# A decoder layer's down projection: Strassen's block products in place of plain ones

## The chip, the cores and the metric

The kernel runs on one core of a Trainium2 chip. Its metric is the device time of one execution in microseconds. Three executions of the kernel before took 1628.73, 1629.14 and 1631.95 us, median 1629.14 us.

## The reference, cut to what matters

One layer of a decoder over 1024 tokens of 1024 channels, all in float32. After an input projection, two head groups (retention and RWKV-7) and an output projection comes the part that changes, and behind it a gated embedding and a last norm:

```python
x = x + mixed @ w_o
hf = rms_norm(x, norm_ffn_w)
x = x + (silu(hf @ w_gate) * (hf @ w_up)) @ w_down      # hidden width 2816
hp = rms_norm(x, norm_ple_w)
x = x + (p @ w_ple_up) * sigmoid(hp @ w_ple_gate)
return rms_norm(x, final_norm_w)
```

## The kernel before

Channels lie on the 128 partitions and tokens along the free axis, in two halves of 512. Every float32 matrix is split into two float32r parts, hi and lo, that add up to it (`split`, L246: ScalarE copies hi, VectorE or GpSimd subtracts it for lo). A product of two such matrices takes three matmuls: hi by hi, hi by lo, lo by hi. All these matmuls are issued at L189, in `mm`. An accumulation (eviction from PSUM into SBUF) is a VectorE addition with one operand in SBUF and one in PSUM.

`dense` (L255) runs over a list of weight tiles of 128 output channels by 1024: it loads each in two pieces of 512 columns by DMA (`st`), splits them into `hi` and `lo` (three buffers each), makes 24 matmuls, and hands the PSUM tile `d` to a `use` function. It yields after every third matmul. The last argument of `dense` (L1124) says which engine makes `lo` of a weight tile: VectorE for all tiles of the tail.

The tail begins when both head groups are done for the second token half. `out1` adds the output projection of the second half to `x1`, the residual, which stays in SBUF from there; `norm1` makes the operand `hT`. In the list of `dense` the last two tiles of the first half (`ffn0`) stand between `out1` and what follows, and `norm1` is called within the first of them. Then `ffn1` runs over the 22 hidden tiles of the second token half, gate and up in turn: 48 matmuls of `d` for each hidden tile. The first half of the hidden layer was made earlier and lies in DRAM (`hd`).

The hidden tiles go in pairs (FC = 2: eleven parts, counted from 0). `chunk` takes a buffer for the part, `fetch` loads and splits both hidden tiles of the first token half and both row tiles of `w_down`, and `up` splits the second half's hidden tiles as they are made. After a part's second `up` comes `down(c, 0)` and `down(c, 1)`: for each of 8 output tiles and each token half 6 matmuls into one PSUM bank `pd`, and one VectorE addition into `x1` at L1116. That is 96 matmuls and 16 additions a part. The last part's first token half is brought forward to the end of the tenth part, so that its norm has time; its second half stands between the products `pg` of the embedding's gate, whose weights `wg` are loaded by `gate_weights` during parts 6 to 9.

What runs when is set by the order in which the program emits instructions; a scheduler then orders each engine's stream by priority and by its own cost model. Each engine works its stream in order, and SyncE (SP) issues all DMAs, in order too.

Of the kernel before, what the change touches and what calls it, by code (L numbers as in the profile page):

```python
# [8 lines left out]
F32 = mybir.dt.float32  # L9
# [7 lines left out]
P = 128  # L17
# [12 lines left out]
# columns of the packed constants  # L30
# [7 lines left out]
# columns of the packed parameter vectors  # L38
# [43 lines left out]
# a group may enter a stage once the group before it has reached another  # L82
# [95 lines left out]
def tile_hybrid_layer(ctx: ExitStack, tc: tile.TileContext, I, out):  # L178
# [7 lines left out]
    def mm(ps, lhsT, rhs, start, stop):  # L186
        n = math.prod(rhs.shape[1:])
        pe[0] += n / 2.4 if rhs.dtype == F32R else 2 * max(107.0, n / 1.2)
        return nc.tensor.matmul(ps, lhsT, rhs, start=start, stop=stop)  # L189
# [55 lines left out]
    # a float32 value as two float32r parts that add up to it exactly  # L245
# [53 lines left out]
    def rsqrt(y, x, tmp):  # L299
        """y = x ** -0.5 in place of x for positive x: a guess from the exponent, then Newton's steps"""  # L300
# [8 lines left out]
    # RMS norm over the channels, which lie on the partitions  # L309
# [39 lines left out]
    # =================== input norm, input projection, RWKV and retention ===================  # L349
    with ExitStack() as s1:  # L350
# [22 lines left out]
        # x times the norm's weights; 1 / rms comes in when the projections leave PSUM  # L373
# [57 lines left out]
        def lerp(h, ps, i, t):  # L431
            """token shift with mu of tile i, token half h"""
# [35 lines left out]
        def low(h):  # L468
            """decay, in-context rate and gate of all heads from their low-rank parts"""
# [14 lines left out]
            # the high part beside the low one: one pass over 128 rows for both  # L484
# [34 lines left out]
        # block-diagonal holders; the zero blocks are written once  # L519
# [33 lines left out]
        def rwkv_group(p, hf):  # L553
            """a pair of heads over 8 chunks of 64 tokens; yields (stage, ns until the next matmuls can start)"""
# [11 lines left out]
            def headsum(ps, t):  # L566
                """sum of t over the channels of a head"""
# [11 lines left out]
            # decay and normaliser  # L579
# [35 lines left out]
            # products inside the chunks  # L615
# [25 lines left out]
            # inverse of the unit triangular blocks of 32 rows  # L641
# [32 lines left out]
            # two chunks at a time, then each head's rows to their place  # L674
# [20 lines left out]
            # merge to 64 rows  # L695
# [16 lines left out]
            # the chunk as an affine map: S' = P_C (M S + Kf V), y = Q S + Hy V  # L712
# [9 lines left out]
            for g in range(2):  # L722
# [8 lines left out]
                # M and Q take the room of their factor  # L731
# [6 lines left out]
            # the state (before P_C, transposed) and the output: [(h, v), (k | t)] of each chunk  # L738
# [18 lines left out]
            # head norm in token-major form, bonus, gate  # L757
# [34 lines left out]
        def retention(h, a):  # L792
            """a head over four chunks of 128 tokens; yields ns until the next matmuls can start"""
# [26 lines left out]
            # the scores take the room of v, the states that of k, the output that of the token-major k  # L820
# [13 lines left out]
            # the state before each chunk  # L834
# [25 lines left out]
            # (qs y - mean) / sqrt(var + eps) with the moments of y  # L860
# [16 lines left out]
        # =================== the dense products in an order that feeds the groups ===================  # L877
# [3 lines left out]
        # the embedding's operands, in the room of the retention  # L881
# [57 lines left out]
        # the last heads' first token half before their second one: the operands of the output projection take its room  # L939
# [13 lines left out]
        def mix_load(h, k):  # L953
            """operands of the output projection, token half h"""
# [38 lines left out]
        def ffn0(f, then=None):  # L993
            """the first token half of the hidden layer, kept in DRAM"""
# [53 lines left out]

        FC = 2
        NC = NF // FC  # L1050

        def ffn1(f):
            c, i = f // FC, f % FC

            def gate(ps):
                if i == 0 and c < NC - 1:
                    chunk()
                if f in tail["gates"]:
                    tail["gates"][f]()
# [3 lines left out]
                if c < NC - 1:  # L1063
                    fetch(c, 2 * i)

            def up(ps):
                h = tail["s"][i]
                t = hold.pop(f)
                V.tensor_tensor(out=t, in0=t, in1=ps, op=ALU.mult)
# [120 lines left out]
    for _ in dg:  # L1190
        pass
# [132 lines left out]
```

## Time and profile before

The page of the profile is that of one execution whose span was 1630.8 us from first to last instruction; the page gives no other time for that execution, and its span lies among the three times above.

| engine | busy us | share of the span |
| --- | --- | --- |
| TensorE (PE) | 1519.8 | 93% |
| its weight loads (PEld, beside PE) | 1237.5 | 76% |
| VectorE (DVE) | 1118.9 | 69% |
| ScalarE (ACT) | 689.5 | 42% |
| GpSimd (POOL) | 286.4 | 18% |

The mean granted clock of TensorE was 0.983 of full speed. The share of busy time is an average over stages with different limits, so each stage has to be read for itself. The tail lies from about 1033 us on.

### The profile page before, as it was taken

What the parts mean: (1) busy time and instruction counts of PE and PEld (TensorE: products, weight loads), DVE (VectorE), ACT (ScalarE), POOL (GpSimd) and SP (SyncE); (2) the same over time, 40 slices, a digit from 0 to 9 for tenths busy, and PEclk for the clock granted to TensorE, in tenths of its full rate; (3) what the DMA queues carried; (4) which work ended last, traced back from release to release, by engine and by line L of the source; (5) the groups of instructions that cost most, each with busy time, mean ns of one, the idle gap of its engine ahead of it and who ended that gap; (6) DMA issues with size and microseconds to landing.
All of it is one profiled execution on the core that took longest, in us unless ns stands there. A gap on an engine that the chain in (4) does not pass through costs nothing.

```text
span 1630.8 us, 21374 instructions
## 1 busy us (share of the span) xinstructions
PE 1519.8 (93%) x7406; PEld 1237.5 (76%) x7406; DVE 1118.9 (69%) x2364; ACT 689.5 (42%) x1383; POOL 286.4 (18%) x232
## 2 busy tenths in 40 slices
PE   7999999998888889889899999999999999999994
PEld 5777778786766668767677778788888888788894
DVE  7669796959798697894955545855555554556776
ACT  6655444443635547354253234522222222224554
POOL 7410111021222123323233320000000000000012
PEclk9999999999999999999999999999999999999997
DMA  6544242333534655243333545422222223321222
GB/s 204 168 160 154 91 130 82 111 119 101 194 118 130 211 162 176 69 150 101 117 124 111 167 144 171 155 93 85 84 85 82 73 79 97 104 78 46 72 84 78
DMA packets 108763, 194.06 MB, mean 119 GB/s; under 512 B 12272, under 2 KB 16496, under 8 KB 108656
## 3 DMA queue, kind: packets, MB, share of 16 engines
q1 hardware_dynamic: 108656, 192.71, 37.1%
q8 instruction: 58, 0.95, 0.2%
q14 instruction: 49, 0.40, 0.1%
HBM read 151.24 MB, written 41.42 MB: 118 GB/s over the span
## 4 chain that ended last, share of the span: by engine, by line
PE 54%; DVE 25%; DMA 8%; ACT 7%; issue 4%; POOL 2%; SPq 1%; DVEq 0%; ACTq 0%; POOLq 0%
PE d L189 30%; PE pd L189 14%; DVE tmp L643 4%; PE pg L189 3%; DVE R L645 3%; POOL lo L248 2%; DMA st<-in_w_in_dram 1%; DMA st<-in_w_up_dram 1%; ACT hi L247 1%; DVE lo L248 1%; DMA st<-mixd 1%; DVE Dm L637 1%; DMA st<-in_w_gate_dram 1%; PE pb L189 1%; PE pkh L189 1%
## 5 line engine op out<-in xcount | busy, mean ns | idle before, releaser
L189 PE MATMUL d<-hT,hi 128*128 128x512 f32 x1408 | 449.7, 399 | 6.5 <-ACT hi L247 4.0
L189 PE MATMUL d<-x,hi 128*128 128x512 f32 x960 | 322.7, 411 | 9.0 <-ACT x L336 6.7
L247 ACT ACTIVATE hi<-st 128x512 fp32r<-128x512 f32 x298 | 187.6, 629 | 314.0 <-PE d L189 142.7
L189 PEld LDWEIGHTS d<-hT,hi 128*128 128x128 f32 x1408 | 261.5, 190 | 57.8 <-ACT hi L247 6.6
L248 POOL TENSOR_TENSOR lo<-st,hi 128x512 fp32r<-128x512 f32 x139 | 194.1, 1397 | 597.6 <-ACT hi L247 529.6
L189 PE MATMUL d<-hT,lo 128*128 128x512 f32 x704 | 278.7, 396 | 2.8 <-POOL lo L248 2.2
L189 PE MATMUL pd<-h 128*128 128x512 f32 x1056 | 241.8, 389 | 0.0
L189 PEld LDWEIGHTS pd<-h 128*128 128x128 f32 x1056 | 198.2, 188 | 41.1
L189 PEld LDWEIGHTS d<-x,hi 128*128 128x128 f32 x960 | 179.1, 194 | 43.6 <-ACT x L336 6.7
L189 PE MATMUL d<-x,lo 128*128 128x512 f32 x480 | 194.0, 404 | 2.3 <-POOL lo L248 2.3
L248 DVE TENSOR_TENSOR lo<-st,hi 128x512 fp32r<-128x512 f32 x159 | 110.7, 697 | 109.4 <-ACT hi L247 108.9
L1116 DVE TENSOR_TENSOR x<-x,pd 128x512 f32<-128x512 f32 x176 | 120.5, 687 | 92.7 <-PE pd L189 91.8
L189 PEld LDWEIGHTS d<-hT,lo 128*128 128x128 f32 x704 | 133.6, 190 | 35.6 <-POOL lo L248 5.0
L247 ACT ACTIVATE h<-xr 128x512 fp32r<-128x512 f32 x66 | 38.4, 624 | 194.6 <-PE pd L189 176.7
L1198 POOL TENSOR_TENSOR x<-x,xr 128x256 f32<-128x256 f32 (+1 forms) x18 | 19.8, 1130 | 561.6 <-DVE xr L328 561.6
L189 PEld LDWEIGHTS d<-x,lo 128*128 128x128 f32 x480 | 93.1, 194 | 22.1 <-POOL lo L248 4.2
L643 DVE TENSOR_TENSOR tmp<-Dt,R 128x248 f32<-128x248 f32 (+30 forms) x248 | 89.8, 362 | 3.2
L645 DVE TENSOR_TENSOR R<-R,tmp 128x248 f32<-128x248 f32 (+30 forms) x248 | 82.7, 334 | 3.3
L189 PE MATMUL d<-mix,hi 128*128 128x512 f32 x256 | 82.1, 400 | 1.6 <-ACT hi L247 1.5
L189 PEld LDWEIGHTS d<-mix,hi 128*128 128x128 f32 x256 | 48.1, 192 | 11.7 <-ACT hi L247 1.9
L248 DVE TENSOR_TENSOR h<-xr,h 128x512 fp32r<-128x512 f32 x66 | 42.8, 689 | 14.0 <-ACT h L247 13.9
L1004 POOL TENSOR_TENSOR g<-g,R 128x512 f32<-128x512 f32 x22 | 29.2, 1325 | 125.6 <-DVE g L1003 122.8
(284 smaller groups left out, 2159.8 us busy)
## 6 DMA issues: line engine op xcount, KB each, us to landing
st<-in_w_gate_dram SPq DMA_DIRECT2D x88, 256.0 KB, 2.9
st<-in_w_up_dram SPq DMA_DIRECT2D x88, 256.0 KB, 2.8
st<-in_w_in_dram SPq DMA_DIRECT2D x86, 256.0 KB, 2.9
xr<-in_w_down_dram SPq DMA_DIRECT2D x44, 256.0 KB, 3.4
retd<-rt SPq DMA_DIRECT2D x32, 256.0 KB, 2.6
rr<-retd SPq DMA_DIRECT2D x32, 256.0 KB, 3.4
st<-in_w_o_dram SPq DMA_DIRECT2D x32, 256.0 KB, 3.0
rkvd<-rkvt SPq DMA_DIRECT2D x24, 256.0 KB, 2.2
```

Source lines behind the costliest of these rows:

```text
L189: return nc.tensor.matmul(ps, lhsT, rhs, start=start, stop=stop)
L247: act(hi, src, AF.Copy)
L248: (eng or V).tensor_tensor(out=lo, in0=src, in1=hi.bitcast(F32), op=ALU.subtract)
L637: V.tensor_tensor(out=Dm, in0=d0v[:, 0].rearrange("p u t -> p t u").unsqueeze(2).broadcast_to([P, 32, 4, NU]), in1=d0v[:, 1].rearrange("p ...
L643: V.tensor_tensor(out=tmp[:, :, 0:i], in0=Dt[:, i:i + 1, 0:i].broadcast_to([P, 8, i]), in1=R[:, :, i:i + 1].broadcast_to([P, 8, i]), op=AL ...
L645: V.tensor_tensor(out=R[:, :, 0:i], in0=R[:, :, 0:i], in1=tmp[:, :, 0:i], op=ALU.subtract)
L1004: G.tensor_tensor(out=g, in0=g, in1=R0[0], op=ALU.mult)
L1116: V.tensor_tensor(out=x1, in0=x1, in1=ps, op=ALU.add)
L1198: (V if b == S and d % 3 < 2 else G).tensor_tensor(out=x1[d][:, a:b], in0=x1[d][:, a:b], in1=R, op=ALU.mult)
```

## The change

Ten of the eleven parts are no longer multiplied plainly but by Strassen's product in Winograd's form. A part's product is taken as 2 by 2 blocks: the two weight rows by two halves of 512 output channels (A0, A1 for the first half, A2, A3 for the second), the two hidden tiles by two token halves (B0, B1 the first half, from DRAM; B2, B3 the second, just made). Seven block products P1 to P7 of sums of these replace eight. A block product is 4 output tiles (`j`) of one 128-row product: 4 units of 3 matmuls. So a part has 28 units, 84 matmuls, each with its own addition into `x1` or into one of eight new accumulators `E` (E0 to E3 for P1, E4 to E7 for P7), which are added into `x1` once, at the end (`shared`). P2, P7 and P3 go on in the PSUM bank of the product before them, after that has been read.

The units no longer stand in a block behind a part's dense products. `period(c)` makes a table of 32 ticks: one for each yield of `dense` within a part. In period c the units of part c - 1 are emitted, one a tick, while the operands of part c are loaded, summed and split: the weights' sums and the lo parts of their seven operands on GpSimd, those of the first token half on VectorE. At the end of the period `hidden(c)` makes the second half's sums and splits on VectorE. Operands live in a ring of eight slots (tiles ring_9689 and ring_9690); rm_9691 and rm_9692 are E, rm_9693 holds B0, B1 and the weight sums A4, A5, rm_9694 holds B2 to B5, and xr0 to xr3 are A0 to A3. The lo parts of every other dense weight tile of the tail are also made on GpSimd.

The last part stays plain. Its first half, the split of the embedding's operand (`hp_split`) and the last units of part 9 are laid out by `last_period`. The embedding's first four gate weights now go into slots of the ring as these come free, the third and fourth after the dense products.

```diff
+        def weights(c):
...
+            return {-24: lambda: dma(out=A[0], in_=I["w_down"][row(0), half(0)]),
+                    -16: lambda: dma(out=A[2], in_=I["w_down"][row(0), half(1)]),
+                    -9: lambda: dma(out=A[1], in_=I["w_down"][row(1), half(0)]),
+                    -5: lambda: dma(out=A[3], in_=I["w_down"][row(1), half(1)]),
+                    0: lambda: (dma(out=B[0], in_=hd[f]), dma(out=B[1], in_=hd[f + 1])),
+                    1: lambda: (part(c, "P1", 0, A[0], G), sums()),
+                    3: lambda: sub(G, A[2], A[0], A[2]),
...
+                    26: lambda: part(c, names(c)[6], 0, A[3] if names(c)[6] == "P4" else A[1], G)}
+        def hidden(c):
+            B = tail["B"]
+            sub(V, B[4], B[2], B[0])
+            sub(V, B[5], B[3], B[4])
+            part(c, "P6", 1, B[5])
+            sub(V, B[2], B[3], B[2])
+            part(c, "P7", 1, B[2])
+            sub(V, B[1], B[5], B[1])
+            for n in names(c)[4:]:
+                part(c, n, 1, {"P5": B[4], "P3": B[3], "P4": B[1]}[n])
+        def unit(c, name, j):
...
+            for n, (w, x) in enumerate(((0, 0), (0, 1), (1, 0))):
+                mm(ps, t[:, 0, w, cd], t[:, 1, x], start=(first and n == 0), stop=(n == 2), more=not first)
...
+            if c == 0 and name in ("P1", "P7"):
+                act(dst, ps, AF.Copy)
+            else:
+                V.tensor_tensor(out=dst, in0=dst, in1=ps, op=ALU.subtract if name == "P4" else ALU.add)
+        def shared(j):
+            V.tensor_tensor(out=E[4 + j], in0=E[4 + j], in1=E[j], op=ALU.add)
+            V.tensor_tensor(out=x1[j + 4][:, half(0)], in0=x1[j + 4][:, half(0)], in1=E[4 + j], op=ALU.add)
+            G.tensor_tensor(out=x1[j][:, half(1)], in0=x1[j][:, half(1)], in1=E[j], op=ALU.add)
+            G.tensor_tensor(out=x1[j + 4][:, half(1)], in0=x1[j + 4][:, half(1)], in1=E[4 + j], op=ALU.add)
+        def period(c):
+            ticks = [[] for _ in range(32)]
+            if c:
+                for u in range(28):
+                    ticks[u].append(lambda u=u: unit(c - 1, names(c - 1)[u // 4], u % 4))
...
-                    for w, x in ((wh, hh), (wh, hl), (wl, hh)):
-                        mm(ps, w, x, start=(n == 0), stop=(n == 3 * FC - 1))
-                        n += 1
-                x1 = tail["x1"][d][:, half(h)]
-                V.tensor_tensor(out=x1, in0=x1, in1=ps, op=ALU.add)
...
-        dg = dense(items, count, done, lambda i: G if 0 < i < ntail and (i < EV0 or i % EVM) else V)
+        dg = dense(items, count, done, lambda i: G if 0 < i < ntail and (i < EV0 or i % EVM) or i > ntail + KT and i % 2 else V)
...
     for _ in dg:
-        pass
+        tick()
```

TensorE before, in the tail, where a part's dense products (`d`) end and its down products (`pd`) begin:

```order
L189 MATMUL d<-hT_9498,lo 128x512
L189 MATMUL d<-hT_9498,hi 128x512 x2
L189 MATMUL d<-hT_9498,lo 128x512
L189 MATMUL pd<-h 128x512 x96
L189 MATMUL d<-hT_9498,hi 128x512 x2
L189 MATMUL d<-hT_9498,lo 128x512
L189 MATMUL d<-hT_9498,hi 128x512 x2
```

TensorE now, at the end of a middle part; a number behind `pd` is the PSUM tile of one output tile. The first row is the last of P1's four units, and the units that follow are P2's, in the same banks:

```order
L189 MATMUL pd_11833<-ring_9690 128x512 x3
L189 MATMUL d_11809<-hT1_9498,hi_11719 128x512 x2
L189 MATMUL d_11809<-hT1_9498,lo_11720 128x512
L189 MATMUL d_11809<-hT1_9498,hi_11763 128x512 x2
L189 MATMUL d_11809<-hT1_9498,lo_11764 128x512
L189 MATMUL d_11809<-hT1_9498,hi_11763 128x512
L189 MATMUL pd_11802<-ring_9689 128x512 x3
L189 MATMUL d_11809<-hT1_9498,hi_11763 128x512
L189 MATMUL d_11809<-hT1_9498,lo_11764 128x512
L189 MATMUL d_11809<-hT1_9498,hi_11763 128x512
L189 MATMUL pd_11813<-ring_9689 128x512 x3
L189 MATMUL pd_11825<-ring_9689 128x512 x3
```

The down products stand in threes between dense ones, and four P1 units (this row and three before it, with three dense matmuls behind each) come ahead of P2.

VectorE before, at the same place (L1069 is gate times up, the h rows are splits of operands):

```order
L1069 TENSOR_TENSOR g<-g,d 128x512
L248 TENSOR_TENSOR lo<-st,hi 128x512
L1116 TENSOR_TENSOR x_9056<-x_9056,pd 128x512
L248 TENSOR_TENSOR h<-g,h 128x512
L1116 TENSOR_TENSOR x_9056<-x_9056,pd 128x512 x15
L248 TENSOR_TENSOR h<-xr_9057,h 128x512
L248 TENSOR_TENSOR h<-xr_9058,h 128x512
L248 TENSOR_TENSOR h<-xr_9059,h 128x512
L248 TENSOR_TENSOR h<-xr_9060,h 128x512
```

VectorE now, at that place (L1225 is gate times up, B3; the L1076 rows are the sums B5, B2 and B1; the ring rows are lo parts; the row of pd_11802 is the eviction of P1's first unit):

```order
L248 TENSOR_TENSOR ring_9690<-rm_9693,ring_9690 128x512
L1225 TENSOR_TENSOR rm_9694<-g_11725,d_11732 128x512
L248 TENSOR_TENSOR lo_11782<-st_11783,hi_11781 128x512
L1076 TENSOR_TENSOR rm_9694<-rm_9694 128x512 x2
L1076 TENSOR_TENSOR rm_9693<-rm_9694,rm_9693 128x512
L248 TENSOR_TENSOR ring_9689<-rm_9694,ring_9689 128x512 x2
L248 TENSOR_TENSOR ring_9690<-rm_9694,ring_9690 128x512
L248 TENSOR_TENSOR ring_9690<-rm_9693,ring_9690 128x512
L1135 TENSOR_TENSOR rm_9691<-rm_9691,pd_11802 128x512
L248 TENSOR_TENSOR lo_11843<-st_11844,hi_11842 128x512
L1135 TENSOR_TENSOR rm_9691<-rm_9691,pd_11813 128x512
L1135 TENSOR_TENSOR rm_9691<-rm_9691,pd_11825 128x512
```

Eight operations with all operands in SBUF now stand between the product of gate and up and the first eviction of P1; before, there was one split ahead of the first L1116.

GpSimd before: behind the last weight split of the dense list nothing stands until the last norm.

```order
L248 TENSOR_TENSOR lo<-st,hi 128x512 x3
L1004 TENSOR_TENSOR g<-g,R_6146 128x512 x3
L1198 TENSOR_TENSOR x_9056<-x_9056,xr_13618 128x512 x8
L1198 TENSOR_TENSOR x_9056<-x_9056,xr_13910 128x256 x8
L1198 TENSOR_TENSOR x_9056<-x_9056,xr_14042 128x256 x2
```

GpSimd now, at the same place (L1086 and the two L1076 rows are the weight sums A4, A5 and A2 of the next part; the lo rows are dense weights):

```order
L248 TENSOR_TENSOR ring_9690<-xr3_9060,ring_9690 128x512
L248 TENSOR_TENSOR lo_11720<-st_11721,hi_11719 128x512
L1086 TENSOR_TENSOR rm_9693<-xr2_9059,xr3_9060 128x512
L1076 TENSOR_TENSOR rm_9693<-rm_9693,xr0_9057 128x512
L1076 TENSOR_TENSOR xr2_9059<-xr0_9057,xr2_9059 128x512
L248 TENSOR_TENSOR ring_9690<-xr0_9057,ring_9690 128x512
L248 TENSOR_TENSOR lo_11764<-st_11765,hi_11763 128x512
L248 TENSOR_TENSOR ring_9690<-xr1_9058,ring_9690 128x512
L1076 TENSOR_TENSOR xr1_9058<-xr1_9058,rm_9693 128x512
L248 TENSOR_TENSOR ring_9689<-rm_9693,ring_9689 128x512
```

The weight sums and splits of the next part are queued just where VectorE has its eight operations, and a dense weight's lo part stands between them.

## Rows read from the trace of the kernel before

**Rows 1.** A 50 us stretch, and nine from 1050: busy us (count) by engine, clock, DMA.

```profile
1450.00:1500.00 50.00, 50.00 (x222) 41.30 (x221) 34.97 (x51) 17.74 (x28) 0.00 (x0) 1.00 0.11 32
sum 450.00, PE 449.73 PEld 369.59 DVE 247.17 ACT 122.13 POOL 0.00; mean PE 49.97 PEld 41.07 DVE 27.46 ACT 13.57 POOL 0.00
```

**Rows 2.** Chain of waits in the tail: start us, length us, engine and tile.

```profile
1101.85 21.76 PE pd L189 x96
1123.61 21.76 PE d L189 x96
```

**Rows 3.** Groups of the tail: shapes, count, busy us, mean ns, idle before.

```profile
L1116 DVE TENSOR_TENSOR x<-x,pd 128x512 f32<-128x512 f32 x176 | 120.5, 687 | 92.7 <-PE pd L189 91.8
L247 ACT ACTIVATE hi<-st 128x512 fp32r<-128x512 f32 x87 | 54.9, 630 | 95.3 <-PE d L189 49.8 <-DMA st<-in_w_up_dram 25.9 <-DMA st<-in_w_gate_dram 14.5
```

**Rows 4.** A part's end, TensorE then VectorE: start us, us [idle before].

```profile
1101.46 0.39 PE L189 MATMUL d<-hT,lo 128*128 128x512 f32 x1
...
1101.89 0.69 DVE L1069 TENSOR_TENSOR g<-g,d 128x512 f32<-128x512 f32 x1 [1.59 <-PE d L189]
1102.49 0.69 DVE L248 TENSOR_TENSOR lo<-st,hi 128x512 fp32r<-128x512 f32 x1
```

**Rows 5.** Four splits of ScalarE in a row, same view.

```profile
1123.65 2.20 ACT L247 ACTIVATE h<-xr 128x512 fp32r<-128x512 f32 x4 [20.40 <-PE pd L189]
```

**Rows 6.** GpSimd, then VectorE, both with operands in SBUF alone, same view.

```profile
22.62 1.75 POOL L248 TENSOR_TENSOR lo<-st,hi 128x512 fp32r<-128x512 f32 x1
24.32 1.71 POOL L316 TENSOR_TENSOR acc<-acc,sq 128x512 f32<-128x512 f32 x1
...
23.13 1.78 DVE L337 SCALAR_TENSOR_TENSOR x<-raw,par,x 128x512 fp32r<-128x512 f32 x1
24.84 1.75 DVE L316 TENSOR_TENSOR acc<-acc,sq 128x512 f32<-128x512 f32 x1
```

**Rows 7.** GpSimd, then VectorE whose first operand d lies in PSUM (38.45).

```profile
38.42 1.30 POOL L316 TENSOR_TENSOR acc<-acc,sq 128x512 f32<-128x512 f32 x1 [0.76 <-ACT sq L314]
...
38.45 0.69 DVE L434 TENSOR_TENSOR pn<-d,R 128x512 f32<-128x512 f32 x1
39.05 1.22 DVE L443 SCALAR_TENSOR_TENSOR rr<-pn,par,rr 128x511 f32<-128x511 f32 x1
```

**Rows 8.** Groups of GpSimd, 600 to 1000 us.

```profile
L816 POOL TENSOR_TENSOR rr<-rr 128x512 f32<-128x512 f32 x8 | 10.3, 1286 | 13.7 <-DVE rmisc L303 7.4 <-DMA rr<-retd 5.0 <-DVE rmisc L307 1.3
```

**Rows 9.** DMA issues of the tail: count, KB each, median us to landing.

```profile
xr<-in_w_down_dram SPq DMA_DIRECT2D x39, 256.0 KB, 3.2
```

**Rows 10.** The tail's start, TensorE, VectorE, GpSimd: start us, us [idle before].

```profile
1033.76 3.79 PE L189 MATMUL pd<-h 128*128 128x512 f32 x16
1039.95 0.70 PE L189 MATMUL d<-hT,hi 128*128 128x512 f32 x2 [2.41 <-DVE g L1011]
...
1021.10 3.35 DVE L328 RECIPROCAL R<-R 128x512 f32<-128x512 f32 x1 [0.71 <-ACT R L327]
...
1039.12 0.69 DVE L1011 SCALAR_TENSOR_TENSOR g<-g,d 128x512 f32<-128x512 f32 x1
...
1026.28 1.73 POOL L1004 TENSOR_TENSOR g<-g,R 128x512 f32<-128x512 f32 x1 [59.85 <-DVE g L1003]
```

**Rows 11.** Gaps of TensorE and what followed: columns as in rows 1.

```profile
426.80:430.10 3.30, 0.09 (x2) 0.06 (x1) 3.30 (x8) 2.13 (x6) 0.38 (x1) 1.00 0.65 191
430.10:434.20 4.10, 4.10 (x14) 3.31 (x15) 3.31 (x5) 3.26 (x7) 1.20 (x2) 0.58 0.62 194
...
693.90:697.00 3.10, 0.36 (x3) 0.32 (x3) 3.10 (x17) 0.00 (x0) 0.96 (x1) 1.00 0.51 169
697.00:700.50 3.50, 3.50 (x14) 3.02 (x13) 2.50 (x21) 0.00 (x0) 0.00 (x0) 0.51 0.00 1
...
1037.50:1040.00 2.50, 0.09 (x2) 0.08 (x1) 2.50 (x5) 1.66 (x3) 0.00 (x0) 1.00 0.36 90
1040.00:1043.50 3.50, 3.50 (x16) 2.91 (x17) 3.46 (x7) 1.27 (x2) 0.61 (x1) 1.00 0.44 155
```

More of the change, by code (lines that the diff above doesn't have):

```diff
@@ L1050, in tile_hybrid_layer, with tick, names, slot @@
         NC = NF // FC
+        todo = []
+        def tick():
+            if todo:
+                for fn in todo.pop(0):
+                    fn()
+        def names(c):
+            return ("P1", "P2", "P6", "P7", "P5", "P3", "P4") if c < NC - 2 else ("P1", "P2", "P6", "P7", "P4", "P5", "P3")
+        def slot(c, n):
+            k = (7 * c + n + 5) % 8
+            return tail["ring"][k // 4][:, k % 4]
+        def pair(c, name):
+            return slot(c, names(c).index(name))
+        def part(c, name, x, src, eng=V):
+            t = pair(c, name)
+            split(src, t[:, x, 0], t[:, x, 1], eng)
@@ new lines, in wide, with last_weights, last_hidden, down @@
+        def wide(n):
+            return slot(NC - 2, n).rearrange("p a b c -> p (a b c)").rearrange("p (z n) -> p z n", z=2)
+        def last_weights(i, j):
+            f, st = NF - FC + i, tail["A"][2 * i + j]
+            load_split(I["w_down"][f * P:(f + 1) * P, half(j)], *(wide(i)[:, z, half(j)] for z in range(2)), st=st, eng=G)
+        def last_hidden(i, h):
+            return slot(NC - 2, 2 + h)[:, i]
+        def down(h, which):
+            for d in which:
+                ps = pse("pd")
+                cd = slice(d * P, (d + 1) * P)
+                for i in range(FC):
+                    for n, (w, x) in enumerate(((0, 0), (0, 1), (1, 0))):
+                        mm(ps, wide(i)[:, w, cd], last_hidden(i, h)[:, x], start=(i == n == 0), stop=(i == FC - 1 and n == 2))
+                x1 = tail["x1"][d][:, half(h)]
+                V.tensor_tensor(out=x1, in0=x1, in1=ps, op=ALU.add)
+                norm_add(tail["accs"][h], tail["sq"](), x1, d == 0)
@@ L1055, in gate @@
             def gate(ps):
[L1056 to L1059, printed above, removed]
+                if f == 0:
+                    tail["ring"] = [slab.tile([P, 4, 2, 2, HS], F32R, tag="s", name="ring") for _ in range(2)]
+                    tail["room"]()
+                    period(0)
                 t = evac("g")
@@ L1062, in gate, with up @@
                 hold[f] = t
+            def up(ps):
+                t = hold.pop(f)
                 if c < NC - 1:
[L1064 to L1069, printed above, removed]
-                split(t, h[:, 0, half(1)], h[:, 1, half(1)])
-                if c < NC - 1:
-                    fetch(c, 2 * i + 1)
-                if i == FC - 1:
-                    if c < NC - 1:
-                        down(c, 0)
-                        down(c, 1)
-                    if c == NC - 2:
-                        chunk()
-                        for step in range(2 * FC - 1):
-                            fetch(NC - 1, step)
-                        down(NC - 1, 0)
+                    V.tensor_tensor(out=tail["B"][2 + i], in0=t, in1=ps, op=ALU.mult)
+                    if i == FC - 1:
+                        while todo:
+                            tick()
+                        hidden(c)
+                        if c < NC - 2:
+                            period(c + 1)
+                        else:
+                            last_period()
+                else:
+                    V.tensor_tensor(out=t, in0=t, in1=ps, op=ALU.mult)
+                    split(t, last_hidden(i, 1)[:, 0], last_hidden(i, 1)[:, 1])
@@ L1157, in tile_hybrid_layer, with room8, room @@
     wg = []
+    def room8(i, shape, name, dtype=F32R):
+        return np2.tile(shape, dtype, tag=f"wg{i}", name=name)
+    def room():
+        q = [room8(i, [P, 4, HS], "rm", F32) for i in range(4)]
+        tail["E"] = [q[i // 4][:, i % 4] for i in range(8)]
+        raw = [q[2 + i // 4][:, i % 4] for i in range(8)]
+        tail["A"] = xrs + raw[:2]
+        tail["B"] = raw[2:]
+        tail["late"] = raw[:2]
     def gate_weights(n):
@@ L1251, in tile_hybrid_layer @@
                 for w, x in ((0, 0), (0, 1), (1, 0)):
[L1252 removed]
+                    mm(ps, wg[d][:, w, c], hps[h][k][:, x, t], start=(i == 0), stop=(i == 23))
                     i += 1
@@ L1267, in tile_hybrid_layer @@
                     split(accs[1], *sums)
-                    hp_split(1)
+                    for e in range(KT):
+                        hp_split(1, e)
             if d == DN:
```

127 lines of the change are left out of this document (87 added, 40 removed).

## The prediction

> **What bounds the kernel now.** I read the stretches of the tail first. From 1050 to 1500 us TensorE is busy 449.73 of 450 us, at full granted clock, VectorE 247 us and GpSimd not at all [rows 1]. Then the chain of waits: it is TensorE alone, 96 dense matmuls in 21.76 us and 96 of the down product in 21.76 us, part after part [rows 2]. So a matmul of 512 columns costs 21.76 / 96 = 0.2267 us, a part 43.52 us, and nothing else sets the end there. Every matmul that goes is worth its price, and every wait of TensorE that comes is paid in full. VectorE has 20 us a part to spare and GpSimd 43; whether they can be used at the same time is the question.
>
> **Matmuls removed.** Ten parts lose 96 - 84 = 12 each: 120 x 0.2267 = 27.2 us. This is the whole gain.
>
> **Work added, on average.** A part now costs VectorE 30 operations with an operand in PSUM (28 evictions, two products of gate and up) and 15 with SBUF operands alone (four sums, seven lo parts, four dense lo parts). An operation lasts 0.687 us [rows 3], but the next starts 0.60 us after it [rows 4], so this is 45 x 0.60 = 27 us. GpSimd gets 15 operations of 1.29 us [rows 8], 19 us. ScalarE gets 24 of 0.63 us [rows 3], 15 us. A part's TensorE time would be 180 x 0.2267 = 40.8 us, so on average all of it is hidden, and the DMAs move the same bytes. What counts is where TensorE waits for an operation that has others ahead of it.
>
> **VectorE and GpSimd exclude each other.** Where both work on SBUF operands alone, they alternate: GpSimd 1.75 and 1.71 us, VectorE 1.78 and 1.75 us [rows 6], against 1.29 and 0.69 alone. A VectorE operation that finds GpSimd at work ends 0.55 us after it (GpSimd ends 24.37, VectorE 24.91), and a GpSimd operation behind a VectorE one ends 1.12 us after that (24.91 to 26.03). An operation that reads PSUM is not held: 0.69 us inside one of GpSimd, while the next, with SBUF operands, took 1.22 us [rows 7]. The Trainium skill's page "SBUF — State Buffer", section "Who interferes with whom", states this as a lock held for the whole instruction, between a VectorE instruction with two SBUF inputs and GpSimd's reads; its section "A bandwidth-pool intuition that's wrong" gives about 115 ns from the holder's end to the loser's start, and a held operation would then end about 0.8 us after GpSimd, 0.25 us later than the rows show. By that figure some 36 collisions would cost 9 us more; the rows decide, and I use 0.55 us.
>
> **The end of a part.** I count from t = 0, the start of P1's first unit, the first matmul after a part's dense ones. TensorE's order has 28 matmuls from there to P2's first unit, so it comes to it at 28 x 0.2267 = 6.35 us. P2 goes on in P1's bank, so it waits for VectorE's eviction of P1, behind eight operations with SBUF operands. The last dense matmul started at -0.23; the product starts 0.43 us after such a start [rows 4], at 0.20, and ends at 0.89.
>
> Without GpSimd: the dense lo part starts at 0.86 (its hi part on ScalarE waits for a buffer that the last dense matmul reads), the sums B5, B2 and B1 at 1.46, 2.06, 2.66; ScalarE, 0.63 us each and 0.52 from start to start [rows 5], keeps ahead; the four lo parts follow at 3.26 to 5.06, P1's eviction at 5.66 ends at 6.35, and TensorE starts 0.14 us later (1039.81 to 1039.95 in [rows 10]): it waits 0.14 us.
>
> With GpSimd: its burst begins when A3 has landed. The buffer of A3 comes free when P4's weights are split, and their slot when P3's last matmul, the fortieth before t = 0, is done: -8.67. ScalarE 0.63, GpSimd 1.29, DMA 3.2 [rows 9] give -3.5. Then come A4 (-3.5 to -2.2), A5 (to -1.0), held up once by the lo part of the next P1 on VectorE (-2.0 to -0.4), A2 (to 0.70), the lo part of P1's weights (0.65 to 1.94), a dense lo part. VectorE's dense lo part therefore ends at 1.94 + 0.55 = 2.49 instead of 1.55; GpSimd's at 2.49 + 1.12 = 3.61 (TensorE needs it at its 26th matmul, 5.9: in time); B5 at 4.16 instead of 2.15; B2 at 4.76, B1 at 5.36. ScalarE makes the hi parts of P6 from 4.19, P7 from 4.79, P4 from 5.39, and P2's weights from 5.91 to 6.54; VectorE's lo parts run from 5.27, 5.87 and 6.47, GpSimd takes P2's weights when that one ends at 7.16, to 8.28, and the last lo part ends at 8.83. P1's eviction ends at 9.44, TensorE starts P2 at 9.58: a wait of 3.2 us, with all of its stream behind it. The next unit waits 0.3 more, since a dense lo part stands between the first two evictions and meets GpSimd's next sum. If the last collision does not fall so, it is 2.2 + 0.5. So 2.7 to 3.5 us, and I take 3.2, for nine part ends (the tenth has no next part to prepare): 28.8 us. With no collision at all it would be 9 x 0.14 = 1.3.
>
> **The clock.** Such a wait is one gap. After gaps of 3.2 and 2.7 us (0.09 us busy of 3.30, 0.36 of 3.10) the granted clock was 0.58 and 0.51 for the next 4 us, that is, at the lower of its two levels, 1.2 for 2.4 GHz, for about 3.4 us, which costs 1.7 us of matmuls; after the 2.4 us gap at 1037.5, in a denser stretch, it stayed at 1.00 [rows 11]. Nine ends: 0 to 15 us. I take three of nine, 5 us.
>
> **The tail's start.** Before, TensorE filled with 16 down matmuls and then sat idle 2.41 us for L1011 on VectorE [rows 10]; now 3 stand there, 13 x 0.2267 = 2.9 us less. Between the reciprocal at 1021.10 and L1011 VectorE had 22 operations and now has 16: 3.7 us less. But GpSimd, which did one operation there, now has ten ahead of and behind L1004, and each can cost a collision of 1.1 us, as the one before shows (1.73 us). So -0.8 to +10; with three collisions +2.5.
>
> **The last period.** `shared` puts eight additions on VectorE and eight on GpSimd, all on SBUF, in front of P4's evictions, whose banks the plain products of part 10 take 48 matmuls (10.9 us) later. VectorE needs 8 us for what stands there without collisions, 16 with one at each: 0 to 6 us, I take 2. Two more gate weights are loaded after the dense products; the third is due two products and two pairs of down tiles later, 72 x 0.2267 = 16 us, and before, four came in 33 us: nothing.
>
> **Sum.** -27.2 + 28.8 + 5 + 2.5 + 2 = +11. The profile's span, 1630.8 us, lies 1.7 us above the median, so I put the difference on the median: 1629 + 11 = 1640 us.
>
> **Rivals.**
> The collisions stay away: the A3 transfer lands earlier or the sums run in the gaps of VectorE's burst, so that P1's eviction is in time. For it speaks that GpSimd is busy only 19 of 41 us; against it that its order puts the sums right behind the last transfer. This ends on the other side: -27.2 + 1.3 - 0.8 = -27, 1603 us. It decides as soon as the wait at a part's end is under 27.2 / 9 = 3.0 us less the other terms, about 2.
> Some collisions: one or two of four, 1.1 us each, 1.5 us a part end and no fall of the clock: -27.2 + 13.5 + 4.5 = -9, 1620 us.
> Everything late: 3.5 us at each end, the clock down each time, ten collisions at the start: -27.2 + 31.5 + 15 + 10 + 4 = +33, 1662 us. Related to it is VectorE as the bound: if all 15 operations of a part collide, 30 x 0.60 + 15 x 1.75 = 44.3 us a part, over the 43.5 of before: 1636 us, within the forecast's own range.
> That the change doesn't do what it says, the matmuls not falling by 120: the order of TensorE has them gone, so I leave it out.
>
> **How the numbers follow.** Forecast (1628 to 1655 by the bounds of its own terms, not all at one end) 0.50; collisions stay away 0.25; some collisions 0.16; everything late 0.09. A difference under 0.2%, 3.3 us, can't be told from none here. Faster: 0.25 and 0.13 of the third case, 0.38; same: 0.03 of it and 0.07 of the forecast, 0.10; slower 0.52. Range: 1604, which leaves out half of the second case's lower side, to 1660.
>
> **What would show it.** Right: in the stretches after, TensorE idle 2 to 4 us once a part, its wait put down to VectorE's L1135; GpSimd's L1086 and L1076 and VectorE's L248 and L1076 at 1.7 us near a part's end; L1135 at 0.69 us; the granted clock under 1.00 in some of those stretches. Wrong: TensorE over 99% busy in the tail with 180 matmuls in 41 us a part, or waits of another kind: for weights (GpSimd's lo of a dense tile), for a DMA, or in the last 130 us.

## The result, and the profile after

The changed kernel took 1653.41 us (median of four executions, 1639.13 to 1657.07) beside 1628.93 of the kernel before: 1.0143 times as long, 95% interval 1.0097 to 1.0190. Run again later, it took 1653.24 us, ratio 1.0142 (1.0117 to 1.0167). So it is slower by 24 us, where 11 were forecast. The execution read here has a span of 1655.3 us, 24.5 more than the one of before; it is the slowest of the four. The page's first part shows 120 matmuls less, as counted, and GpSimd's time nearly doubled:

```profile
PE 1511.1 (91%) x7286; PEld 1226.3 (74%) x7286; DVE 1240.8 (75%) x2460; ACT 729.2 (44%) x1451; POOL 532.4 (32%) x404
```

Stretches of 50 us, with the columns of [rows 1], and the sum of all nine from 1050 us. TensorE was busy 449.73 of these 450 us and is now 425.85; the clock is under 1.00 in seven of the nine (one row shown).

```profile
1200.00:1250.00 50.00, 45.13 (x186) 36.49 (x184) 38.09 (x51) 16.14 (x28) 23.28 (x17) 0.93 0.27 80
...
sum 450.00, PE 425.85 PEld 346.70 DVE 336.86 ACT 146.55 POOL 214.22; mean PE 47.32 PEld 38.52 DVE 37.43 ACT 16.28 POOL 23.80
```

What TensorE waited for between 1045 and 1488 us (us in total, times, longest) is one line, and it is VectorE's eviction of P1, once a part, at eight part ends:

```profile
PE pd L189 <- DVE rm L1135: 21.8, 8, 2.9
```

**One such end.** VectorE, GpSimd and TensorE of the changed kernel around 1385 us (start us, us, count). The product that [rows 4] shows as L1069 is now L1225; behind it stand a dense lo part, three sums (L1076), four lo parts, and then P1's eviction L1135.

```profile
1379.18 0.69 DVE L1225 TENSOR_TENSOR rm<-g,d 128x512 f32<-128x512 f32 x1 [1.09 <-PE d L189]
1379.78 1.27 DVE L248 TENSOR_TENSOR lo<-st,hi 128x512 fp32r<-128x512 f32 x1
1380.97 2.97 DVE L1076 TENSOR_TENSOR rm<-rm 128x512 f32<-128x512 f32 x3
1383.87 3.55 DVE L248 TENSOR_TENSOR ring<-rm,ring 128x512 fp32r<-128x512 f32 x4
1387.34 0.68 DVE L1135 TENSOR_TENSOR rm<-rm,pd 128x512 f32<-128x512 f32 x1
```

```profile
1379.20 1.30 POOL L248 TENSOR_TENSOR ring<-xr,ring 128x512 fp32r<-128x512 f32 x1
1380.46 1.73 POOL L248 TENSOR_TENSOR lo<-st,hi 128x512 fp32r<-128x512 f32 x1
1385.21 1.66 POOL L248 TENSOR_TENSOR ring<-xr,ring 128x512 fp32r<-128x512 f32 x1 [3.02 <-ACT ring L247]
```

```profile
1388.07 1.65 PE L189 MATMUL pd<-ring 128*128 128x512 f32 x3 [2.59 <-DVE rm L1135]
```

GpSimd's operations that end at 1380.50, 1382.19 and 1386.87 each hold one of VectorE up: VectorE's dense lo part ends at 1381.05, its first sum (1380.97 to 1382.74) 0.55 us after GpSimd's second, its last lo part (1385.67 to 1387.42) 0.55 us after the third. That is 0.58 + 1.08 + 1.07 = 2.7 us more than 0.69 each. The eviction itself, which reads PSUM, takes 0.68 us beside GpSimd.

**The same end without GpSimd** stands in the same execution: part 9 has no next part to prepare, so GpSimd does nothing from 1467.6 to 1473.7 us.

```profile
1468.55 0.69 DVE L1225 TENSOR_TENSOR rm<-g,d 128x512 f32<-128x512 f32 x1 [2.78 <-PE d L189]
1469.16 0.68 DVE L248 TENSOR_TENSOR lo<-st,hi 128x512 fp32r<-128x512 f32 x1
1469.76 1.90 DVE L1076 TENSOR_TENSOR rm<-rm 128x512 f32<-128x512 f32 x3
1471.57 2.50 DVE L248 TENSOR_TENSOR ring<-rm,ring 128x512 fp32r<-128x512 f32 x4
1473.97 1.29 DVE L1135 TENSOR_TENSOR rm<-rm,pd 128x512 f32<-128x512 f32 x2
```

From the product to P1's eviction it is 5.42 us here and 8.16 at 1379: 2.74 us, about the gap of 2.59 us there. TensorE has no gap here.

**The clock.** Two of the ten stretches from 1036 to 1528 us in which TensorE had half its clock (0.50, that is 1.2 GHz), and the sum of all ten. Seven begin at a part end.

```profile
1111.16:1117.98 6.82, 6.02 (x14) 0.50 0.27 79
...
1387.63:1391.05 3.42, 2.98 (x7) 0.50 0.51 145
...
sum 47.80, PE 42.12; mean PE 4.21
```

In the ten, 98 matmuls started in 42.12 us of busy time (a count in a row takes in those that were still running when its stretch began); at 0.2267 us each they are 22.2 us, so 19.9 us are lost, 14.7 of them at the part ends. Before, the tail ran at 1.00 from 1040 to 1600 us.

**The tail's start and the last period.** TensorE's wait for L1011 is 5.59 us, before 2.41 [rows 10]; GpSimd's operations ahead of L1011's end run at up to 2.04 us, but VectorE also sits idle for 1.90 us there, behind a hi part whose weight had not landed. In the last period, from 1488 us, TensorE waits 6.8 us in all, three of its four lines shown; before, it had no gap over 0.2 us there:

```profile
1038.60 1.19 PE L189 MATMUL d<-hT,hi 128*128 128x512 f32 x2 [5.59 <-DVE g L1011]
...
1025.26 1.05 DVE L248 TENSOR_TENSOR lo<-st,hi 128x512 fp32r<-128x512 f32 x1 [1.90 <-ACT hi L247]
...
1029.80 2.04 POOL L248 TENSOR_TENSOR lo<-st,hi 128x512 fp32r<-128x512 f32 x1 [4.04 <-ACT hi L247]
```

```profile
PE nrm L189 <- ACT sq L247: 2.3, 1, 2.3
PE pd L189 <- DVE x L1181: 2.2, 2, 1.2
PE pd L189 <- DVE rm L1135: 2.0, 2, 1.8
```

### The profile page after: what moved, and what is told of

It reads as the page before. It is cut to its first block, busy times and chain, and to the rows that moved or that the text cites. A ratio compares the mean times of both kernels' runs of the same rounds, so it can differ in the third digit from the quotient of the medians.

```text
span 1655.3 us, 21602 instructions
## 1 busy us (share of the span) xinstructions
PE 1511.1 (91%) x7286; PEld 1226.3 (74%) x7286; DVE 1240.8 (75%) x2460; ACT 729.2 (44%) x1451; POOL 532.4 (32%) x404
## 4 chain that ended last, share of the span: by engine, by line
PE 48%; DVE 29%; DMA 8%; ACT 7%; issue 5%; POOL 4%; SPq 0%; DVEq 0%; ACTq 0%; POOLq 0%
PE d L189 26%; PE pd L189 11%; DVE tmp L643 4%; PE pg L189 3%; DVE R L645 3%; POOL lo L248 2%; DVE ring L248 2%; DVE lo L248 2%; DMA st<-in_w_up_dram 1%; DVE rm L1076 1%; ACT hi L247 1%; DMA st<-mixd 1%; DVE Dm L637 1%; DMA st<-in_w_in_dram 1%; DMA st<-in_w_gate_dram 1%
## 5 line engine op out<-in xcount | busy, mean ns | idle before, releaser
L248 POOL TENSOR_TENSOR lo<-st,hi 128x512 fp32r<-128x512 f32 x185 | 261.3, 1414 | 611.2 <-ACT hi L247 552.1
L189 PE MATMUL pd<-ring 128*128 128x512 f32 x936 | 270.9, 405 | 26.4 <-DVE rm L1135 23.8
L189 PEld LDWEIGHTS pd<-ring 128*128 128x128 f32 x936 | 182.3, 196 | 71.2 <-DVE rm L1135 26.6
L1135 DVE TENSOR_TENSOR x<-x,pd 128x512 f32<-128x512 f32 x200 | 133.5, 683 | 59.4 <-PE pd L189 59.0
L248 DVE TENSOR_TENSOR lo<-st,hi 128x512 fp32r<-128x512 f32 x113 | 98.5, 872 | 51.2 <-ACT hi L247 50.8
L248 POOL TENSOR_TENSOR ring<-xr,ring 128x512 fp32r<-128x512 f32 x54 | 75.1, 1394 | 182.7 <-ACT ring L247 121.7
L247 ACT ACTIVATE ring<-rm 128x512 fp32r<-128x512 f32 x92 | 57.1, 630 | 145.4 <-PE pd L189 60.3
L247 ACT ACTIVATE ring<-xr 128x512 fp32r<-128x512 f32 x54 | 33.6, 628 | 114.6 <-PE pd L189 114.6
L248 DVE TENSOR_TENSOR ring<-rm,ring 128x512 fp32r<-128x512 f32 x72 | 74.8, 1073 | 5.5 <-ACT ring L247 4.6
L1135 DVE TENSOR_TENSOR rm<-rm,pd 128x512 f32<-128x512 f32 x72 | 47.6, 681 | 21.5 <-PE pd L189 21.5
```

The source lines that it names most:

```text
L247: act(hi, src, AF.Copy)
L248: (eng or V).tensor_tensor(out=lo, in0=src, in1=hi.bitcast(F32), op=ALU.subtract)
L1135: V.tensor_tensor(out=dst, in0=dst, in1=ps, op=ALU.subtract if name == "P4" else ALU.add)
```

## The experiments

The theory: VectorE's burst at a part's end is lengthened by GpSimd's work, P1's eviction comes late, TensorE waits, and the clock falls after the wait. The rivals are that VectorE simply has too much to do there, and that the clock falls for another reason than the gap. Each time is a median; each ratio is to the kernel before on the same chip, with its 95% interval.

**Filling the gaps.** In `dense`, behind the fourth column of a gate product that follows a part end:

```diff
...
+                    if i in refill and a == 3:
+                        for b in range(4):
+                            bh, bl = parts[i, 0]
+                            cb = slice(b * P, (b + 1) * P)
+                            for m, (w, x) in enumerate(((bh, xs[b][0]), (bh, xs[b][1]), (bl, xs[b][0]))):
+                                mm(ps, w[:, cb], x, start=(b == m == 0), stop=False)
...
```

> At eight of the nine part ends TensorE gets 12 more matmuls ahead of P2's first unit: the first four columns of the dense product that stands there are computed once more from the start (the sum then goes on as before, so the output is the same). 96 matmuls x 0.2267 = 21.8 us of work that serves nothing. Theory (the wait of P2 for P1's eviction makes a gap, and the gap makes the clock fall): the extra matmuls stand in the gaps of 2.6 to 2.9 us, the wait put down to L1135 falls from 23.8 to under 5 us, the granted clock stays at 1.00 after these ends, and the 34 us that the changed kernel spends there at half clock come back as 17 us: about 1636 us (1630 to 1642), with 96 matmuls more than the changed kernel. Rival A (the clock falls because of how the tail's work is mixed, with GpSimd busy, not because of the gap): the clock falls go on, 1653 us. Rival B (the eviction is late because it waits for TensorE's progress, so that the gap moves with it): the gaps stay, 1653 + 21.8 = 1675 us.

Measured: 1649.36 us, ratio 1.0127 (1.0113 to 1.0142). In this kernel P1's eviction stands at L1141.

```profile
PE pd L189 <- DVE rm L1141: 8.3, 8, 1.3
```

None of the eight ends is followed by a fall of the clock any more; there is no stretch at half clock between 1046 and 1600 us. So at these ends it is the gap that brings the fall, and rival A is out. The time is 13 us above what I expected and outside the range. Some 8 of the 13 are gaps that stayed, since they only shrank from 2.7 to 1.0 us: TensorE's order now has 36 matmuls from P1's first unit to P2's first, where it had 28 (8 more, not 12), and at the end I looked at, VectorE's burst took 8.67 us to P1's eviction, 0.5 more. Another 2 are that the falls there had cost 14.7 us and not the 17 that I gave back. The kernel is 4 us faster than the changed kernel with 96 matmuls, 21.8 us of work, added.

**GpSimd's work on VectorE.** All sums and lo parts of `weights`, and the dense lo parts:

```diff
-                G.tensor_tensor(out=A[4], in0=A[2], in1=A[3], op=ALU.add)
+                V.tensor_tensor(out=A[4], in0=A[2], in1=A[3], op=ALU.add)
...
-                    5: lambda: part(c, "P2", 0, A[1], G),
+                    5: lambda: part(c, "P2", 0, A[1]),
...
-        dg = dense(items, count, done, lambda i: G if 0 < i < ntail and (i < EV0 or i % EVM) or i > ntail + KT and i % 2 else V)
+        dg = dense(items, count, done, lambda i: G if 0 < i < ntail and (i < EV0 or i % EVM) else V)
```

> The weights' lo parts and sums and the dense lo parts of the tail go from GpSimd to VectorE; GpSimd keeps only the last period and the tail's start's L1004. VectorE gets 15 more operations a part, 60 x 0.60 = 36 of 41 us. Theory (GpSimd holds VectorE up by exclusion): with more work on VectorE the burst at a part's end is shorter, eight operations at 0.60 us, P1's eviction is in time, the waits for L1135 at the nine ends fall from 2.7 us to under 0.5, the clock stays at 1.00 there: 1653 - 22 (waits) - 17 (clock) = 1614 us (1606 to 1622). Rival (VectorE simply has too much to do in that stretch): the 15 operations more make P1's eviction later by up to 4 x 0.6 us, waits of 3 to 5 us an end, 1655 to 1680 us.

Measured: 1615.62 us, ratio 0.9916 (0.9903 to 0.9930). With 156 instructions more on VectorE the kernel is 38 us faster than the changed one. The waits from 1045 to 1440 us, and one part end on VectorE:

```profile
PE pd L189 <- DVE rm L1135: 3.1, 8, 0.7
```

```profile
1264.42 1.90 DVE L1076 TENSOR_TENSOR rm<-rm 128x512 f32<-128x512 f32 x3
1266.22 2.50 DVE L248 TENSOR_TENSOR ring<-rm,ring 128x512 fp32r<-128x512 f32 x4
1268.63 0.68 DVE L1135 TENSOR_TENSOR rm<-rm,pd 128x512 f32<-128x512 f32 x1
```

The burst has 0.60 us from start to start again, the waits at the eight ends are 0.2 to 0.7 us, and none is followed by a fall of the clock. The rival, that VectorE has too much to do, is out.

**Four ticks later.** GpSimd keeps its work:

```diff
-                    ticks[u].append(lambda u=u: unit(c - 1, names(c - 1)[u // 4], u % 4))
+                    ticks[u + 4].append(lambda u=u: unit(c - 1, names(c - 1)[u // 4], u % 4))
...
-                    ticks[at].append(fn)
+                    ticks[at + 4].append(fn)
...
-                        ticks[32 + at].append(fn)
+                        ticks[36 + at].append(fn)
```

> The units of a period and the work on its weights are put four ticks later against the dense products (ticks u + 4 for u, weights from 0 on four later, those ahead of the period four later too), so that 12 dense matmuls stand ahead of P1's first unit after the burst of the hidden sums. GpSimd keeps its work. Theory: P2's first unit comes 12 x 0.2267 = 2.7 us later after the burst, so the wait of 2.6 to 2.9 us at each part end falls to under 0.5 us, and the clock stays at 1.00 there: 1653 - 22 - 17 = 1614 us (1606 to 1622); what the collisions cost VectorE then costs nothing. Rival (P4's evictions and GpSimd's sums move with the units, so that the burst ends later by as much): waits of 1 to 3 us stay, 1630 to 1655 us.

Measured: 1671.54 us, ratio 1.0263 (1.0249 to 1.0277): slower still. The rival is right in kind, but its 1 to 3 us of waiting and its range to 1655 us are too small. The waits to 1480 us, and one part end on VectorE and GpSimd:

```profile
PE pd L189 <- DVE rm L1135: 33.8, 8, 4.7
```

```profile
1385.41 0.69 DVE L1225 TENSOR_TENSOR rm<-g,d 128x512 f32<-128x512 f32 x1
1386.02 1.13 DVE L248 TENSOR_TENSOR ring<-rm,ring 128x512 fp32r<-128x512 f32 x1
1387.08 1.78 DVE L248 TENSOR_TENSOR lo<-st,hi 128x512 fp32r<-128x512 f32 x1
1388.78 2.98 DVE L1076 TENSOR_TENSOR rm<-rm 128x512 f32<-128x512 f32 x3
1391.68 0.68 DVE L248 TENSOR_TENSOR lo<-st,hi 128x512 fp32r<-128x512 f32 x1
1392.29 4.62 DVE L248 TENSOR_TENSOR ring<-rm,ring 128x512 fp32r<-128x512 f32 x4
1396.83 1.87 DVE L1135 TENSOR_TENSOR rm<-rm,pd 128x512 f32<-128x512 f32 x3
```

```profile
1386.56 1.75 POOL L1076 TENSOR_TENSOR xr<-xr,xr 128x512 f32<-128x512 f32 x1
1388.27 1.74 POOL L248 TENSOR_TENSOR ring<-xr,ring 128x512 fp32r<-128x512 f32 x1
1393.31 1.39 POOL L248 TENSOR_TENSOR ring<-xr,ring 128x512 fp32r<-128x512 f32 x1 [3.30 <-ACT ring L247]
```

GpSimd's sums moved into the burst with the units (the sum A2 starts 1.15 us behind the product; in the changed kernel it starts 1.68 us ahead of it), and two lo parts more stand in VectorE's queue there: from the product to P1's eviction it is 11.42 us. TensorE comes to P2 8.06 us after the product (1393.47), before 6.31, so it gains 1.75 and loses 3.26. Each of the eight gaps of 4.0 to 4.7 us was followed by 6.8 us at half clock.

**Both edits.**

> Both edits at once: four ticks later, and GpSimd's work of the tail on VectorE. Theory: either edit alone takes the wait away, so both together give nothing more than the better one: 1612 us (1604 to 1620), no gap over 0.5 us at the part ends. Rival (each takes away only a part of the wait): 10 us or more under the better of the two.

Measured: 1607.47 us, ratio 0.9870 (0.9855 to 0.9886). No gap is left at a part end. The time is 8 us under that of the better edit: in the range, and between the theory (nothing more) and the rival (10 us or more). Of the 9.1 us between the two profiled executions 5.1 lie ahead of the tail's wait for `hT` (the `d` matmul behind it starts at 1036.42 with one edit and 1031.33 with both), where I did not follow them; the other 4.0 are hardly more than the 3.1 us of waits that the part ends still had. The shift that cost 18 us beside GpSimd costs nothing without it.

**Which half of GpSimd's work.** Once only `weights` goes to VectorE, once only the dense lo parts, by the lines above.

> Only the weights' sums and lo parts go to VectorE; the dense lo parts of the odd products stay on GpSimd. In the changed kernel three collisions lengthen the burst of a part's end by 0.58 (a dense lo part, 1.27 us), 1.08 (a hidden sum, 1.77 us, behind GpSimd's dense lo part) and 1.07 us (the last lo part, 1.75 us, behind P2's weights), 2.73 together, and the gap is 2.6 to 2.9. Theory: the first and third go with the weights, the second stays: a wait of about 1.1 us (0.5 to 1.7) at each of the eight part ends, too short to bring the clock down, 1653 - 8 x 1.6 - 17 = 1623 us (1616 to 1632), above the 1615.6 of the kernel with nothing on GpSimd. Rival (one collision of the three is the cause and the others are covered): the wait is either gone (1614) or unchanged (1653).

> The other half: only the dense lo parts of the odd products go to VectorE, the weights' sums and lo parts stay on GpSimd. Theory: of the three collisions the second goes (1.08 us), and GpSimd's queue is shorter by the dense lo part, so that its sums end earlier; the wait falls to 1.6 us (1.0 to 2.3) at each part end, the clock still falls after some: 1653 - 8 x 1.1 - (0 to 17) = 1636 us (1626 to 1646). Rival as for the other half: gone (1614) or unchanged (1653).

Measured: 1616.51 us, ratio 0.9918 (0.9895 to 0.9940), for the weights; 1639.81 us, ratio 1.0068 (1.0043 to 1.0093), for the dense lo parts. Waits with the weights on VectorE, 1045 to 1440 us; then, with the dense lo parts there, two gaps of equal length and the 3.4 us after each, columns of [rows 1]:

```profile
PE pd L189 <- DVE rm L1135: 2.6, 8, 0.5
```

```profile
1291.23:1293.61 2.38, 0.01 (x1) 0.01 (x1) 2.38 (x4) 0.60 (x1) 2.30 (x2) 1.00 0.06 22
1293.61:1297.00 3.39, 3.38 (x13) 2.46 (x14) 3.39 (x6) 0.63 (x1) 0.47 (x1) 1.00 0.52 155
1335.03:1337.40 2.37, 0.00 (x1) 0.00 (x0) 2.37 (x4) 0.48 (x1) 2.29 (x2) 0.99 0.00 1
1337.40:1340.80 3.40, 3.40 (x8) 2.72 (x9) 3.40 (x5) 0.63 (x1) 0.48 (x1) 0.50 0.47 154
```

Both times lie in their ranges, but neither wait is the one forecast, so that is in part luck. Without the weights on GpSimd its dense lo part has nothing ahead of it and runs from 1343.53 to 1344.99 us, before the product at 1346.07, so the second collision goes with the first and third: 0.3 us of wait, not 1.1. Without the dense lo parts the second collision goes, as I said: P1's eviction starts 6.98 us after the product (1329.69 to 1336.67), 1.18 sooner. But the product itself is late: it starts 1.16 us behind P1's first unit (1328.53), in the changed kernel 0.20 us (1378.98 to 1379.18), because two lo parts ahead of it on VectorE, the second a dense one that the changed kernel does not have there, take 1.78 us each beside GpSimd's sums:

```profile
1326.29 1.78 DVE L248 TENSOR_TENSOR ring<-rm,ring 128x512 fp32r<-128x512 f32 x1 [0.27 <-ACT ring L247]
1327.99 1.78 DVE L248 TENSOR_TENSOR lo<-st,hi 128x512 fp32r<-128x512 f32 x1
```

So TensorE, with the same 28 matmuls between P1's and P2's first units, comes to P2 5.34 us after the product, before 6.31, and the wait is 2.4 us at six ends (1.3 at two), not 1.6. The weights on GpSimd are what the loss needs: with them on VectorE 37 of the 38 us come back, with the dense lo parts there 14. The two shares overlap, since the second collision goes with either half. And of these six equal gaps four were followed by a fall of the clock.

**A shorter burst.** GpSimd keeps all its work:

```diff
...
-            for n in names(c)[4:]:
-                part(c, n, 1, {"P5": B[4], "P3": B[3], "P4": B[1]}[n])
...
+        def rest(c, k):
+            B, n = tail["B"], names(c)[4 + k]
+            part(c, n, 1, {"P5": B[4], "P3": B[3], "P4": B[1]}[n])
...
+                    ticks[6 + 2 * k].append(lambda k=k: rest(c - 1, k))
```

> GpSimd keeps all its work and the units their places; of the burst that follows the hidden layer's product, the lo parts of P5, P3 and P4 are put off (to ticks 6, 8 and 10 of the next period, where they are needed from tick 16 on; the loads of the first token half and the lo parts of P1 and P2 made from them go later, to ticks 11, 16 and 17, since they use the same rooms). In VectorE's order two operations with SBUF operands less stand ahead of P1's eviction, the one that took 1.75 us among them. Theory (what counts is what is ahead of P1's eviction in VectorE's order, and an operation that reads PSUM is not held): P1's eviction starts 0.6 + 1.7 us earlier, the wait is 0.3 us (0 to 1.0), the clock stays at 1.00 there: 1653 - 8 x 2.3 - 17 = 1618 us (1611 to 1630). Rival (an eviction beside GpSimd's work is late whatever stands ahead of it): the wait stays over 2 us, 1640 us or more.

Measured: 1627.64 us, ratio 0.9995 (0.9980 to 1.0011): 26 us off the changed kernel, none from the kernel before. One part end (the product is L1234 here, P1's eviction L1141), and the waits from 1045 to 1450 us:

```profile
1359.43 0.69 DVE L1234 TENSOR_TENSOR rm<-g,d 128x512 f32<-128x512 f32 x1 [1.00 <-PE d L189]
1360.04 1.35 DVE L248 TENSOR_TENSOR lo<-st,hi 128x512 fp32r<-128x512 f32 x1
1361.31 2.97 DVE L1076 TENSOR_TENSOR rm<-rm 128x512 f32<-128x512 f32 x3
1364.21 1.28 DVE L248 TENSOR_TENSOR ring<-rm,ring 128x512 fp32r<-128x512 f32 x2
1365.42 1.87 DVE L1141 TENSOR_TENSOR rm<-rm,pd 128x512 f32<-128x512 f32 x3
```

```profile
PE pd L189 <- DVE rm L1141: 9.9, 8, 1.4
```

P1's eviction starts 5.99 us after the product instead of 8.16, as expected; but TensorE's order now has P2's first unit 24 matmuls behind P1's, four fewer, so it comes 0.9 us earlier and still waits 1.2. After none of these eight gaps did the clock fall.

**No GpSimd in the last period.** On top of both edits:

```diff
-            G.tensor_tensor(out=x1[j][:, half(1)], in0=x1[j][:, half(1)], in1=E[j], op=ALU.add)
-            G.tensor_tensor(out=x1[j + 4][:, half(1)], in0=x1[j + 4][:, half(1)], in1=E[4 + j], op=ALU.add)
...
+        def shared1(j):
+            x1, E = tail["x1"], tail["E"]
+            V.tensor_tensor(out=x1[j][:, half(1)], in0=x1[j][:, half(1)], in1=E[j], op=ALU.add)
...
-            ticks[24].append(lambda: tail["hp0"]())
+            ticks[28].append(lambda: tail["hp0"]())
...
+                ticks[13 + v].append(lambda v=v: shared1(v))
...
```

> The kernel four ticks later with the tail's work on VectorE (1607.5 us), and the last period too without GpSimd: the eight additions of it go to VectorE, one a tick from tick 13, the lo parts of the last weights and of the first gate weights too, and the norm's sum of the first token half is taken four ticks later. Theory: of the gaps left in the last period (2.42, 0.20, 0.99 us for evictions behind the shared additions, 1.84 us for the norm's sum) 4 to 5 us go, and the two falls of the clock after them, 2 x 1.7 us: 1599 us (1595 to 1605). Rival (VectorE, with some 14 operations more in 30 us, is late for the evictions of the plain products): new gaps of as much, 1606 us or more.

Measured: 1596.72 us, ratio 0.9802 (0.9778 to 0.9827): 32 us faster than the kernel before, the fastest version. From 1040 to 1575 us TensorE waits once:

```profile
PE nrm L189 <- ACT xr L247: 0.7, 1, 0.7
```

This edit does two things at once, and no run parts them: it takes GpSimd out of the last period, and it puts the norm's sum later. In the changed kernel GpSimd stood idle from 1507.6 us on, so the waits there for L1181 and for the norm's sum (1514 to 1523 us) were not collisions.

**The changed kernel again.**

> The changed kernel once more, as it is, since its first four times lie 18 us apart (1639 to 1657). Theory (the waits are the same in each execution, and what differs is after how many of them the clock falls): gaps of 2.6 to 2.9 us at the same eight part ends again, a different set of falls of the clock after them, a median between 1640 and 1656 us. Rival (the waits themselves differ from one execution to the next): gaps of other lengths or at other places in this profile.

Measured: 1653.24 us. The waits to 1480 us:

```profile
PE pd L189 <- DVE rm L1135: 22.1, 8, 3.0
```

They are at the same eight ends, 2.5 to 3.0 us long. The clock fell after four of them, for 3.4 us (once 6.8), where it had fallen after seven, and half clock cost 11.9 us in all instead of 19.9: the waits belong to the program, the falls to the execution.

## Why the prediction was right in kind and short in size

The forecast, slower through the wait of P2 for P1's eviction, is what happened; the time is 13 us above it.

- **Matmuls removed:** 120, 27.2 us, as counted. The kernel that ends at 1596.7 us has all of it: its tail, from the first matmul with `hT` to the last norm's, took 581.7 us, before 608.7. What it gains beyond that lies ahead of the tail, where even the two profiled executions of the changed kernel differ by 3.3 us (the tail's first matmul at 1007.92 and 1011.19).
- **A part's end:** +28.8 forecast (nine of 3.2 us), +21.8 measured (eight of 2.73). The ninth was my error: of the part that comes first P1 goes out on ScalarE, so nothing waits. The chain was right at its ends (8.55 us from the product to the eviction's start by my count, 8.16 in the trace), and inside too: three operations of VectorE are held, the dense lo part, the first sum and the last lo part, for 2.73 us where I had 3.1. Without GpSimd I gave 0.14 us; 0 at part 9, and 0.2 to 0.7 us where VectorE has all the work.
- **The clock:** +5 forecast, 19.9 measured, and 11.9 in the second execution. This is the term that was mis-sized most. I took three falls in nine, since one gap of 2.4 us had left the clock up [rows 11]; after gaps of 2.5 to 3.0 us it fell 7 times in 8 and then 4 in 8, some falls lasted 6.8 us and not 3.4, and the start and the last period added three. The upper end of 15 that I gave was for the part ends alone, where 14.7 and 7.5 us were lost.
- **The tail's start:** +2.5 forecast; 5.59 - 2.41 = 3.2 there, and two small gaps ahead of it (0.8 and 0.6 us), 4.6 together, in its range. I had only collisions in this term; that VectorE also waited 1.90 us for a weight I had not, so that the size fits is in part luck.
- **The last period:** +2 forecast, 6.8 measured, above the 6 that I gave as its end. I had priced the shared additions, and the evictions behind them cost 2.3 us; the norm's sum (2.3 us) and the plain products' evictions (2.2 us), which also wait, I had not.

Together -27.2 + 21.8 + 19.9 + 4.6 + 6.8 = 25.9 us. The tail took 608.7 us before (1011.54 to 1620.25) and 637.2 now (1007.92 to 1645.07), 28.4 more; ahead of it this execution was 3.6 us shorter, behind it 0.3, which makes the 24.5. So 2.5 us of the tail stand in none of my terms. My estimate is that they are what a stop costs beyond its idle time: at the part end at 1430.57 us, where the clock stayed up, 20 matmuls around a gap of 2.81 us took 3.42 us more than 20 x 0.2267. I did not count it for every gap.

The Trainium skill's page "SBUF — State Buffer", section "Who interferes with whom", has the exclusion as the trace shows it. The held VectorE operations end 0.55 us after GpSimd's again (1382.19 to 1382.74), as in [rows 6]; an estimate from the about 115 ns of that page's section "A bandwidth-pool intuition that's wrong" would put their end 0.25 us later, so it does not hold for this pair.

Of the signs named beforehand, the wait on L1135, times near 1.7 us on GpSimd (L1076) and VectorE (L248 and L1076), L1135's 0.68 us and the clock under 1.00 came; GpSimd's L1086 did not, it kept 1.29 us. The rival "collisions stay away" (1603 us) did not happen. The runs bracket its price: with the parts' work taken from GpSimd the kernel takes 1616 us, and 1597 with the units four ticks later and the last period changed too.

## What to carry to other kernels

An idle engine is only free if it can work beside the busy one: some 15 small operations a part on GpSimd cost 38 us more than the same operations on a VectorE that was already 75% busy, where 3.1 us of waits were left at the part ends. Count what stands in a queue ahead of the one operation that the bounding engine waits for, at the place where it waits, and not the average load. And price a short gap in a dense stream with what comes after it: here 2.7 us of waiting cost another 1.4 to 2.9 us at half clock, at four of the eight ends in one execution and at seven in the other.

## What the runs showed that I had not expected

- Whether the clock falls after a gap is not settled by its length alone. At the part ends it fell after none of 18 gaps of 0.8 to 1.4 us, four of six of 2.4 us, 11 of 16 of 2.5 to 3.0 us, and all eight of 4.0 to 4.7 us. What decides between equal gaps stays open.
- An edit on VectorE's work alone also moved TensorE's order: P2's first unit stood 28 matmuls behind P1's in the changed kernel and 24 in the kernel with the shorter burst, 0.9 us of wait by itself.
- Work moved off GpSimd can be held up earlier in VectorE's queue instead: with only the dense lo parts on VectorE its burst was 1.18 us shorter, but the product ahead of the burst came 0.96 us later, and at six of the eight ends the wait hardly changed (2.4 us, where it had been 2.6 to 2.9).
